# A tuned transformer kernel on one core: placing the side engines by a simulated timeline instead of the scheduler's default clock

## The chip, the cores and the metric

The kernel runs on one core of one Trainium2 chip. The metric is the device time of one execution in microseconds (us). Before the change the median of three timed runs is 2640.34 us (2638.31 to 2640.6). The profiled execution, from which every row below comes, took 2637.59 us; its span from the first to the last instruction is 2635.8 us.

## The reference

The input is 512 tokens of width 1024. The computation, all in fp32:

```
first block, on 16 meta tokens + 512 tokens:
  h = rmsnorm(x); split h @ w_in into the parts of
    FoX : 8 heads of 64, causal, softmax(q k^T * scale + cum[q] - cum[k]), times silu(gate)
    MLA : low-rank q (256) and kv (128), 8 heads, rope, chunk mask, softmax, times silu(gate)
  x = x + rmsnorm(concat(FoX, MLA) @ w_out)
two hybrid layers:
  h = rmsnorm(x); proj = h @ w_in
  A: mLSTM, 4 heads of 128, both directions, with a gate and a norm
  B: grouped-query attention, 8 query and 2 key heads of 64, rms norm of q and k, axial rope
  C: neighbourhood attention, 8 heads of 64, with a bias table
  D: differential attention, 4 heads, value width 128
  merged = sum over A..D of sigmoid(h @ w_gl) * (y @ w_up);   x = x + merged @ w_out
  x = x + (silu(h2 @ w_gate) * (h2 @ w_up)) @ w_down     with inner width 2816
final rms norm
```

## The kernel before

**Numbers.** Every operand of a large product is split into a high and a low half (`hi`, `lo`; `whi`, `wlo` for weights; `pth`, `ptl` for transposed attention maps), and a product is three TensorE passes: hi x whi, hi x wlo, lo x whi (`mm3` and its kin, L248 to L250, L296 to L298). So each weight tile of 128x512 that arrives by DMA (`raw`) passes two side engines before TensorE can use it, in `split_w`:

```
A_.copy(hi, src)                                                              # L220, ScalarE
k.turn += 1
(V if k.lo and k.turn % k.lo == 0 else G).tensor_tensor(lo, src, f(hi), ALU.subtract)   # L222
```

The subtraction is on GpSimd, except while branch B's queries are projected (`k.lo = 2`), where VectorE has every second one. `evict_split` does the same for results in PSUM: the cast on ScalarE (L210, L213), the subtraction on VectorE (L211, L214).

**Stages, in order of time (us of the span).** 0 to 34: loads, first norm (`norm_tile`, L503, L309, L310, L527) and its transposes. 34 to 200: projections and FoX. 200 to 308: MLA. 308 to 372: w_out of the first block with its two norms. 372 to 1470: layer 1 (A to about 540, B to 700, C to 870, D and merging to 1188, FFN after that). 1470 to 2636: layer 2, the same.

**The order of TensorE is written out by hand.** The whole body runs under `with tc.manual_schedule(engines={mybir.EngineType.PE})`: TensorE's instructions stand in the order in which the Python code issues them. `overlap` interleaves the stages of an attention map (scores, softmax, transposes, product with the values) with projection work from a `Stream` queue, by lags and credits (`LAG_F`, `LAG_M`, `TAIL`, `BETWEEN`, L32 to L40, L128). So the projection work is the filler under which a map's softmax runs on the side engines.

**The order of the other engines is not written out.** The tile framework's scheduler takes the instructions of VectorE (DVE), ScalarE (ACT), GpSimd (POOL) and SyncE (SP, which issues all large DMAs) and decides which comes next on each engine; an engine then runs its own list strictly in that order, and waits at the first instruction whose input is missing, with all that stand behind it. The scheduler's idea of when things are ready decides who stands ahead of whom.

**What the prediction's steps touch.** FoX: `p = A + cb` (L922, two pieces when the map is wider than 512), softmax (L331 max, L332 exp on ACT, L333 reciprocal), scale (L923), then transposes (L314), `pth`/`ptl` (L210, L211), product with the values (L443); after every second head `pair_out` (copy L446, two DMAs L452/L453, adds L454/L455), the gate (L931) and `split_y` (L459 ACT, L460 POOL). The score matmul (L721) of a later map takes over the PSUM bank that an earlier L922 has read. MLA: scale on ACT (L963) or DVE (L965), gate L977. First block's output: L1006, L1010, then `norm_tile`. Branch A: mask add L1336 and a power L1383 on POOL, normalisation L1378 to L1384. Branch B: norm and rope of the queries, `norm_rope` L1459 to L1468 with L309/L310, combination L1513/L1514; the merging `x = (g+1) * A` (L1148) of branch A's output runs beside it. Branch C: bias DMA L1630, bias add on POOL L1631, map L1636 to L1638, output split L1644/L1645, key stacks by DMA L390/L391.

The function that the change touches, and what calls it:

Of the kernel before, what the change touches and what calls it, by code (L numbers as in the profile page):

```python
# [1838 lines left out]
def build(nc, arrays):  # L1839
    aps = {}  # L1840
    for name, a in arrays.items():
        aps[name] = nc.dram_tensor(f"in_{name}_dram", a.shape, mybir.dt.from_np(a.dtype), kind="ExternalInput").ap()
    out = nc.dram_tensor("out_0_dram", (S, D), F32, kind="ExternalOutput").ap()
    with tile.TileContext(nc) as tc:
        hybrid_kernel(tc, aps, out)


# [9 lines left out]
```

## Time and profile before

| | before |
|---|---|
| median of three runs | 2640.34 us (2638.31 to 2640.6) |
| profiled execution, own time | 2637.59 us |
| its span | 2635.8 us |
| outside the span | 1.79 us |
| mean granted TensorE clock | 0.989 |
| TensorE busy | 2554.8 us, 97% |
| VectorE, ScalarE, GpSimd busy | 51%, 44%, 49% |
| DMA, mean over the span | 105 GB/s |

TensorE is busy for 97% of the span, so the time can change in two ways only: TensorE's waits (81 us in all, the span less its busy time) become shorter or longer, or the stretches in which its clock is granted at half change in number. The side engines are half idle on average, so their busy time says little; what counts is when single instructions of theirs end.

### The profile page before, as it was taken

Reading aid. Unit: us, or ns where it says so; the run is one execution under the profiler, and the core shown is the slowest. Engines: PE = TensorE matmul, PEld = TensorE weight load, DVE = VectorE, ACT = ScalarE, POOL = GpSimd, SP = SyncE. Lnnn points to the kernel's source line nnn. Section 1 sums busy time; section 2 is a strip of 40 time slices with the busy share of each in tenths; the row PEclk is TensorE's granted clock in tenths of the full one; section 3 lists DMA queues with packets and bytes.
Section 4 is the critical chain, followed back from the end, with each engine's and each line's share of the span. In section 5 each row is a group of like instructions: output and inputs, shape, how many; then the busy total and the mean of one; then the engine's idle time right before and its main releaser. Section 6 shows DMA issues by size and latency. Waiting matters only on the chain.

```text
span 2635.8 us, 36300 instructions
## 1 busy us (share of the span) xinstructions
PE 2554.8 (97%) x12918; PEld 2127.0 (81%) x12918; DVE 1334.6 (51%) x2895; ACT 1162.8 (44%) x2533; POOL 1291.5 (49%) x1112
## 2 busy tenths in 40 slices
PE   7999989999999999999999999999999999999998
PEld 7878778778887887788888887888888877888887
DVE  3677547858536466432222368685364573322223
ACT  4567645436534445332222454365454453322223
POOL 3443345442465543545555555524655535455554
PEclk9999999999999999999999999999999999999999
DMA  4542232222436332422222332223364233222222
GB/s 144 143 130 69 82 125 97 70 77 72 135 112 180 114 104 81 144 81 96 96 96 96 109 110 69 83 73 103 122 182 127 94 91 139 85 96 96 96 96 88
DMA packets 117732, 276.96 MB, mean 105 GB/s; under 512 B 15824, under 2 KB 37584, under 8 KB 117552
## 3 DMA queue, kind: packets, MB, share of 16 engines
q1 hardware_dynamic: 117552, 274.65, 33.2%
q8 instruction: 102, 1.67, 0.3%
q14 instruction: 78, 0.64, 0.1%
HBM read 230.26 MB, written 6.46 MB: 90 GB/s over the span
## 4 chain that ended last, share of the span: by engine, by line
PE 75%; DVE 10%; POOL 4%; issue 4%; DMA 3%; ACT 2%; SPq 0%; POOLq 0%; DVEq 0%; ACTq 0%
PE A L248 17%; PE A L249 16%; PE A L250 16%; PE A L296 5%; PE A L297 5%; PE A L298 5%; PE A L314 4%; PE A L443 3%; POOL wlo L222 2%; DMA raw<-in_w_out_dram 1%; DVE ptl L211 1%; DMA cb<-in_c_rpb_z_dram 1%; PE A L488 1%; DVE sm L331 1%; PE A L278 1%
## 5 line engine op out<-in xcount | busy, mean ns | idle before, releaser
L222 POOL TENSOR_TENSOR wlo<-raw,whi 128x512 fp32r<-128x512 f32 (+2 forms) x721 | 926.7, 1288 | 903.1 <-ACT whi L220 894.8
L220 ACT CAST whi<-raw 128x512 fp32r<-128x512 f32 (+2 forms) x733 | 443.9, 608 | 777.6 <-PE A L249 447.4
L248 PE MATMUL A<-hi,whi 128*128 128x512 f32 (+1 forms) x1848 | 744.3, 403 | 0.4 <-ACT hi L210 0.4
L250 PE MATMUL A<-hi,wlo 128*128 128x512 f32 (+1 forms) x1848 | 725.7, 393 | 10.3 <-DVE wlo L222 5.8
L249 PE MATMUL A<-lo,whi 128*128 128x512 f32 (+1 forms) x1848 | 727.0, 393 | 0.4 <-DVE lo L211 0.4
L250 PEld LDWEIGHTS A<-hi,wlo 128*128 128x128 f32 x1848 | 349.7, 189 | 91.0 <-DVE wlo L222 7.5
L248 PEld LDWEIGHTS A<-hi,whi 128*128 128x128 f32 x1848 | 350.4, 190 | 66.2 <-ACT whi L220 0.9
L249 PEld LDWEIGHTS A<-lo,whi 128*128 128x128 f32 x1848 | 350.3, 190 | 64.2 <-DVE lo L211 0.6
L314 PE MATMUL A<-ident,p 128*128 128x128 f32 (+3 forms) x1125 | 175.5, 278 | 28.1 <-DVE p L527 19.9
L497 DVE TENSOR_TENSOR x<-x,A 128x512 f32<-128x512 f32 x176 | 120.0, 688 | 154.0 <-PE A L298 96.8
L314 PEld LDWEIGHTS A<-ident,p 128*128 128x128 f32 (+3 forms) x1125 | 135.7, 139 | 67.2 <-DVE p L527 19.1
L211 DVE TENSOR_TENSOR ptl<-A,pth 128x512 fp32r<-128x512 f32 (+3 forms) x256 | 148.9, 583 | 80.0 <-ACT pth L210 78.9
L332 ACT ACTIVATE p<-p,sm 128x512 f32<-128x512 f32 (+6 forms) x160 | 100.7, 629 | 155.2 <-DVE sm L331 154.0
L354 DVE SCALAR_TENSOR_TENSOR t<-t,A 128x512 f32<-128x512 f32 x44 | 30.3, 688 | 252.7 <-ACT t L353 252.7
L210 ACT CAST pth<-A 128x512 fp32r<-128x512 f32 (+3 forms) x256 | 127.5, 502 | 54.6 <-PE A L314 54.2
L310 POOL TENSOR_TENSOR rstd<-rstd,mhalf 128x1 f32<-128x1 f32 (+2 forms) x80 | 56.0, 701 | 194.4 <-DVE rstd L309 187.8
L296 PE MATMUL A<-whi,hi 128*128 128x256 f32 (+7 forms) x440 | 145.9, 332 | 0.0
L297 PE MATMUL A<-wlo,hi 128*128 128x256 f32 (+7 forms) x440 | 143.1, 325 | 1.1 <-POOL wlo L222 1.1
L298 PE MATMUL A<-whi,lo 128*128 128x256 f32 (+7 forms) x440 | 142.9, 325 | 0.0
L1067 DVE SCALAR_TENSOR_TENSOR t<-A,t 128x512 f32<-128x512 f32 x44 | 30.4, 692 | 171.2 <-PE A L250 171.2
L296 PE MATMUL A<-whi,yh 128*128 128x512 f32 x288 | 112.1, 389 | 0.0
L297 PE MATMUL A<-wlo,yh 128*128 128x512 f32 x288 | 112.1, 389 | 0.0
(365 smaller groups left out, 4563.3 us busy)
## 6 DMA issues: line engine op xcount, KB each, us to landing
raw<-in_t_gl_dram SPq DMA_DIRECT2D x64, 512.0 KB, 3.5
raw<-in_t_gate_dram SPq DMA_DIRECT2D x44, 512.0 KB, 3.4
raw<-in_t_up_dram SPq DMA_DIRECT2D x44, 512.0 KB, 3.4
raw<-in_w_ffn_down_dram SPq DMA_DIRECT2D x44, 512.0 KB, 3.7
raw<-in_w_in_dram SPq DMA_DIRECT2D x26, 512.0 KB, 3.5
raw<-in_w_out_dram SPq DMA_DIRECT2D x24, 512.0 KB, 3.5
ks<-sth SPq DMA_DIRECT2D x64, 128.0 KB, 2.4
ks<-stl SPq DMA_DIRECT2D x64, 128.0 KB, 2.4
```

The source lines that it names most:

```text
L210: A_.copy(hi, ps)
L211: V.tensor_tensor(lo, ps, f(hi), ALU.subtract)
L220: A_.copy(hi, src)
L222: (V if k.lo and k.turn % k.lo == 0 else G).tensor_tensor(lo, src, f(hi), ALU.subtract)
L248: T_.matmul(ps, sh, mh, start=first, stop=False)
L249: T_.matmul(ps, sh, ml, start=False, stop=False)
L250: T_.matmul(ps, sl, mh, start=False, stop=last)
L296: T_.matmul(ps, sh, wh[:, j], start=(b + j == 0), stop=False)
L297: T_.matmul(ps, sh, wl[:, j], start=False, stop=False)
L298: T_.matmul(ps, sl, wh[:, j], start=False, stop=(b + j == nk - 1))
L314: T_.transpose(dst, src, ident[0:k, 0:k])
L497: V.tensor_tensor(xx, xx, ps, ALU.add)
```

## The change

One argument of the tile framework's context. With it the scheduler orders the instructions of the engines other than TensorE by a simulated timeline of engines and queues, where it went by its default clock before.

```
@@ -1841,7 +1841,7 @@
     out = nc.dram_tensor("out_0_dram", (S, D), F32, kind="ExternalOutput").ap()
-    with tile.TileContext(nc) as tc:
+    with tile.TileContext(nc, schedule_with_timeline_sim=True) as tc:
         hybrid_kernel(tc, aps, out)
```

No arithmetic changes. TensorE's list is the same, instruction for instruction. On the other engines the same operations stand in another order, over the whole program; on SP the order of some DMA issues changes too.

First place, VectorE in branch B of layer 1 (about 572 to 581 us of the trace). `wlo_6700` is the low half of a weight tile that TensorE's L250 waits for; `cb_6543` are queries in `norm_rope`; `x_4403` is the merged output; a row with + is new at this place, one with - has left it.

```order
 L1461 TENSOR_REDUCE bss_6649<-t_1402_6647 128x8
+L222 TENSOR_TENSOR wlo_6700<-raw_6697,whi_6699 128x512
 L309 TENSOR_SCALAR rstd_6651<-bss_6649 128x8
+L1148 SCALAR_TENSOR_TENSOR x_4403<-sth_4920,A_6636 128x512
 L1463 TENSOR_TENSOR cb_6543<-cb_6543,rstd_6651 128x512
-L1148 SCALAR_TENSOR_TENSOR x_4403<-t_1036_4919,A_6618 128x512
 L1464 TENSOR_TENSOR t_1401_6646<-cb_6543,cst_6067 128x512
 L1467 TENSOR_TENSOR t_1402_6647<-cb_6543,cst_6067 128x8x16 x4
-L222 TENSOR_TENSOR wlo_6700<-raw_6697,whi_6699 128x512
```

The subtraction L222 moves from behind L1463 to L1467 to a place ahead of L309. Layer 2 has the same piece with other numbers.

Second place, VectorE in FoX (about 148 to 155 us). `p_1835` is the map whose L922 frees a PSUM bank; the rows of `t_353` and `t_358` (L810 to L815) are the low-rank projections of MLA. Before:

```order
L309 TENSOR_SCALAR rstd_1768<-lss_1762 128x1
L815 TENSOR_SCALAR t_353_1759<-t_353_1759,rstd_1768 128x256
L211 TENSOR_TENSOR ptl_1687<-A_1749,pth_1686 128x4x128
L810 TENSOR_TENSOR t_359_1781<-t_358_1780,rope_774 128x16
L309 TENSOR_SCALAR rstd_1785<-lss_1783 128x1
L810 TENSOR_TENSOR t_359_1781<-t_358_1780,rope_774 128x16 x3
L815 TENSOR_SCALAR t_358_1780<-t_358_1780,rstd_1785 128x128
L309 TENSOR_SCALAR rstd_1789<-lss_1783 128x1
```

These eight rows stood one behind the other ahead of L922 of `p_1835`, with six more between the last of them and it. Now, at the same place:

```order
L309 TENSOR_SCALAR rstd_1764<-lss_1762 128x1
L211 TENSOR_TENSOR yl_171<-A_1689,yh_170 16x256
L309 TENSOR_SCALAR rstd_1768<-lss_1762 128x1
L922 TENSOR_TENSOR p_1835<-A_1831,cb_1661 128x400
L810 TENSOR_TENSOR t_359_1781<-t_358_1780,rope_774 128x16 x4
L815 TENSOR_SCALAR t_353_1759<-t_353_1759,rstd_1764 128x128
```

L922 of `p_1835` now stands directly behind the first of the eight; the low-rank work follows it.

Third place, ScalarE at the end of MLA (about 297 to 305 us). `p_3863` is the last map but one that L963 scales; `qs_3879` is the split of a gated head pair, whose input comes from L455 and L977 on VectorE.

```order
-L210 CAST yh_170<-A_3826 16x256
+L459 CAST qs_3879<-t_837_3873 128x512
 L210 CAST pth_3889<-A_3891 128x128
 L210 CAST yh_170<-A_3892 16x256
@@ -408,9 +410,8 @@
 L345 ACTIVATE p_3863,smb_3864<-A_3858,smb_3864 128x264
 L446 COPY t_845_3915<-A_3882 128x512
+L210 CAST pth_3917<-A_3919 128x3x128
 L963 ACTIVATE p_3863<-p_3863,smb_3864 128x528
-L459 CAST qs_3879<-t_837_3873 128x512
```

Here the cast L459, which has to wait for the gated pair, moves from behind L963 of `p_3863` to a place ahead of that map's casts and exponentials, and a cast of another map (`pth_3917`) moves ahead of L963.

## Rows read from the trace of the kernel before

**Rows 1.** Busy time of the engines on the page: us, share, instructions.

```profile
PE 2554.8 (97%) x12918; PEld 2127.0 (81%) x12918; DVE 1334.6 (51%) x2895; ACT 1162.8 (44%) x2533; POOL 1291.5 (49%) x1112
```

**Rows 2.** TensorE's waits: instruction <- releaser: us in total, times, longest us.

```profile
PE A L314 <- DVE p L527: 19.9, 9, 7.7
...
PE A L250 <- DVE wlo L222: 5.8, 2, 2.9
...
PE A L250 <- POOL wlo L222: 4.5, 2, 2.3
PE A L721 <- DVE p L922: 3.4, 2, 2.0
...
PE A L278 <- ACT whi L220: 1.2, 1, 1.2
...
PE A L278 <- POOL wlo L222: 0.9, 1, 0.9
```

**Rows 3.** TensorE's timeline, branch B, layer 1: start, duration, [idle before <- releaser].

```profile
580.98 0.50 PE L250 MATMUL A<-hi,wlo 128*128 128x512 f32 x1 [2.90 <-DVE wlo L222]
```

**Rows 4.** Timeline of ScalarE, the same stretch.

```profile
572.07 1.12 ACT L220 CAST whi<-raw 128x512 fp32r<-128x512 f32 x2
```

**Rows 5.** Timeline of VectorE, the same stretch.

```profile
576.54 1.77 DVE L1463 TENSOR_TENSOR cb<-cb,rstd 128x512 f32<-128x512 f32 x1 [2.86 <-POOL rstd L310]
...
580.24 0.68 DVE L222 TENSOR_TENSOR wlo<-raw,whi 128x512 fp32r<-128x512 f32 x1
...
586.22 0.69 DVE L1463 TENSOR_TENSOR yn<-yn,rstd 128x512 f32<-128x512 f32 x1 [1.91 <-POOL rstd L310]
```

**Rows 6.** Timeline of GpSimd, the same stretch.

```profile
576.48 1.29 POOL L222 TENSOR_TENSOR wlo<-raw,whi 128x512 fp32r<-128x512 f32 x1
```

**Rows 7.** PE, PEld, DVE, ACT, POOL busy (x count) by stretch, clock, DMA.

```profile
582.00:585.40 3.40, 3.40 (x13) 3.03 (x12) 2.24 (x6) 2.38 (x5) 1.83 (x2) 0.50 0.56 205
155.30:162.10 6.80, 6.80 (x22) 5.14 (x21) 4.66 (x15) 3.52 (x10) 1.19 (x1) 0.50 0.40 108
...
224.00:231.00 7.00, 6.39 (x45) 6.31 (x45) 6.14 (x23) 4.76 (x16) 1.70 (x2) 1.00 0.18 61
1715.20:1718.60 3.40, 3.40 (x13) 2.92 (x14) 3.12 (x7) 2.34 (x5) 0.84 (x1) 0.50 0.62 212
```

**Rows 8.** Timeline of TensorE in FoX.

```profile
148.24 0.61 PE L721 MATMUL A<-ks,qs 128*128 128x400 f32 x2
...
154.87 0.51 PE L721 MATMUL A<-ks,qs 128*128 128x264 f32 x2 [1.96 <-DVE p L922]
```

**Rows 9.** Timeline of VectorE in FoX, the same place.

```profile
154.24 0.57 DVE L922 TENSOR_TENSOR p<-A,cb 128x400 f32<-128x400 f32 x1
```

**Rows 10.** Timeline of VectorE at the end of FoX.

```profile
189.92 0.49 DVE L923 TENSOR_SCALAR p<-p,sm 128x528 f32<-128x528 f32 x1
...
193.68 1.52 DVE L931 SCALAR_TENSOR_TENSOR t<-t,yn 128x512 f32<-128x512 f32 x1
195.13 0.43 DVE L922 TENSOR_TENSOR p<-A,cb 128x272 f32<-128x272 f32 x1
```

**Rows 11.** Timeline of TensorE at the end of FoX.

```profile
195.61 1.37 PE L721 MATMUL A<-ks,qs 128*128 128x264 f32 x4 [1.46 <-DVE p L922]
```

**Rows 12.** Timeline of VectorE at the end of MLA.

```profile
304.06 0.67 DVE L977 SCALAR_TENSOR_TENSOR t<-t,yn 128x512 f32<-128x512 f32 x1
```

**Rows 13.** Timeline of ScalarE at the end of MLA.

```profile
304.27 0.74 ACT L963 ACTIVATE p<-p,smb 128x528 f32<-128x528 f32 x1
```

**Rows 14.** Timeline of TensorE at the end of MLA.

```profile
305.06 0.71 PE L314 MATMUL A<-ident,p 128*16 128x128 f32 x5 [0.87 <-ACT p L963]
```

**Rows 15.** Timeline of GpSimd in branch A of layer 1.

```profile
487.66 1.27 POOL L460 TENSOR_TENSOR ks<-t,ks 128x512 fp32r<-128x512 f32 x1
```

**Rows 16.** Timeline of GpSimd in branch C of layer 1.

```profile
857.68 1.58 POOL L1645 TENSOR_TENSOR yl<-t,yh 128x512 fp32r<-128x512 f32 x1 [2.58 <-ACT yh L1644]
```

**Rows 17.** Timeline of TensorE in branch C of layer 1.

```profile
857.49 0.40 PE L250 MATMUL A<-hi,wlo 128*128 128x512 f32 x1
```

More of the change, by code (lines that the diff above doesn't have):

```diff
@@ L1843, in build @@
     out = nc.dram_tensor("out_0_dram", (S, D), F32, kind="ExternalOutput").ap()
-    with tile.TileContext(nc) as tc:
+    with tile.TileContext(nc, schedule_with_timeline_sim=True) as tc:
         hybrid_kernel(tc, aps, out)
```

## Prediction

> **What bounds the kernel now.** I read the page first. TensorE is busy for 2554.8 of 2635.8 us [rows 1]; no other engine is above half, so the only time that an order of the side engines can move is the 81 us in which TensorE stands, and what its clock loses beside them. Then the list of TensorE's waits [rows 2]: it says which instruction waits for which, and so which place of which engine's order matters. The largest sums are norm tiles (L527: 19.9 us in nine waits, one of them 7.7 us at the very start, where the input still arrives), the low halves of weights made by L222 on VectorE (5.8 us in two waits) and on GpSimd (4.5 in two), and FoX's L922 (3.4 in two). Two at the start, for the first weights, are 1.2 and 0.9 us. Last I read the timelines of the waiting engine and of its releaser side by side, to see whether the releaser was late because its input was late or because it stood behind other work. Only the second kind can be won.
>
> **The clearest term: branch B, both layers.** TensorE's L250 starts at 580.98 after an idle time of 2.90 us [rows 3]. The cast of that weight's high half was done at 573.2: 572.07 + 1.12 [rows 4]. But VectorE made the low half at 580.24 [rows 5], because L1463 (576.54, after waiting for GpSimd's power) and what follows it stood ahead. In the new order L222 stands ahead of L309, so it can run at about 573.3 and end at 574.0; even if it took as long as the slow L1463, 1.77 us, it would end at 575.1. TensorE wants it at 578.1 (580.98 - 2.90). The wait goes: -2.9 in each layer, as the wait list counts two of them, 2.9 the longest. What was hidden before and might come out: L222's old place is ahead of nothing urgent, and L1148, which also moves forward (0.68 us class, like L222), fills time in which L1463 waits 2.86 us for GpSimd anyway. Bounds for the pair: 0 to -5.8.
>
> From 582.00 to 585.40 and from 1715.20 to 1718.60 the granted clock is 0.50, that is 1.2 of 2.4 GHz, with TensorE busy all the time [rows 7]; it had stood for 2.9 us just before either. The same work at the upper level takes half as long, so each such stretch costs 1.7 us. Not every stretch with idle time has it: 224 to 231 shows 1.00 although TensorE stands for 0.61 us of it. Here I take both stretches as gone: 2 x -1.7 = -3.4, bounds 0 and -3.4. Branch B in all: -9.2, and +0.5 for its attention maps, where the maximum L331 of a later map now stands ahead of a scale.
>
> At this place the Trainium skill speaks against the move. The trace first: L1463 takes 1.77 us when it starts 0.06 us behind GpSimd's L222 (576.48, 1.29 us), and 0.69 alone [rows 5, 6]; it ends 0.5 us after GpSimd's does. The page "SBUF — State Buffer" (section "SBUF: two separate sides") says that VectorE operations with two SBUF inputs and GpSimd share one port pair as an exclusive lock, where the loser waits for the whole instruction. The trace agrees with it here. By that rule a subtraction that VectorE takes earlier can also hold up GpSimd's, and I make a rival of it below; for this place the 3 us to spare cover one such wait of 1.08 us (1.77 - 0.69).
>
> **FoX at 155 us.** L721 starts at 154.87 after 1.96 us idle [rows 8], released by L922, which ran at 154.24 [rows 9]. Its input, the score matmul L721 at 148.24 with a mask behind it [rows 8], was there some 5 us earlier; thirteen rows of low-rank work, output splits and the like stood ahead of it, and in the new order they stand behind it. -2.0. From 155.30 to 162.10 the clock is 0.50 [rows 7]: another -3.4 if it goes too. Bounds 0 to -5.4; I take -5.4.
>
> **End of FoX: a loss.** L922 of `p_2342` moves forward here as well, and the idle 1.46 us before L721 at 195.61 [rows 11] would go. But what L922 passes is the scale L923 of `p_2268` (0.49, at 189.92) and that of `p_2302`, and the latter comes to stand behind L931, which took 1.52 [rows 10]. L931 (193.68 before) would run at about 194.2 to 195.7, with one L923 and a maximum more ahead of it; the scale of `p_2302` (0.3) ends at 196.0, its transposes (0.7, as in rows 14) at 196.7, and only then comes L721: +1.1 against 195.61. An earlier map's scale moves behind an L922 (0.43) and a maximum: +0.6. Together +1.7, with -1.5 (only the wait goes) and +3.5 (all scales wait in a row) as bounds.
>
> **End of MLA: a loss.** ScalarE's L459 must wait for L977, which ended at 304.73 [rows 12], and now stands ahead of the last maps' casts and exponentials. L977 has itself moved forward on VectorE, to an end at about 303.2 by the operations that it passes. Behind it on ScalarE then come a cast of 0.6, and what ran from 301.30 to 304.27 before L963 [rows 13]: packed, about 2.5 us. L963 starts at about 306.4 in place of 304.27, and the transposes at 305.06 [rows 14] come 2.1 later. Bounds: 0 if L977 is done before 301, and +4.1 if it is not earlier than before (304.73 + 0.6 + 3.0 - 304.27). Smaller shifts of the same kind in MLA, four of half a microsecond against two waits of a quarter that go: +0.5. A wait of over 2 us on TensorE was followed by a half-clock stretch in branch B, so I add one: +1.7. MLA in all +4.3.
>
> **Branch A, both layers.** GpSimd's L222 for the L250 that waits (4.5 us, two times) now goes ahead of L460 (1.27 at 487.66) [rows 15]; its own cast and a power ahead of it keep some of that: -0.9 each, bounds 0 and -1.27. Against this, the normalisation L1378 to L1381 is now spread between the reciprocal and the scales of later maps: +0.5 in each layer. Sum -0.8.
>
> **Start.** The two first casts of weights and their low halves go ahead of three casts of activations; L278 waits 1.2 and 0.9 us for them [rows 2]. Two subtractions (0.68 class) slip ahead of the first norms, which I put at +0.5. -1.6, bounds 0 and -2.1.
>
> **First block's output norms.** Two subtractions and two products go ahead of one norm tile and behind the next. I take 0, bounds plus and minus 2.2, the mean of the nine waits (19.9 / 9).
>
> **Branch C.** The bias DMAs are issued ahead of eight key-stack DMAs, and the bias adds follow; but GpSimd's output split, L1645, now stands ahead of a weight's L222. L1645 ran from 857.68 to 859.26 [rows 16], and the L250 that needs that weight started at 857.49 [rows 17]. Unless L1645 itself comes earlier, the low half is ready at 859.26 + 1.29 = 860.55, 3.1 late. Its input hangs on a pair sum that the earlier bias lets come sooner, by about as much; I take +0.5 for each layer, bounds -0.5 and +3.1.
>
> **Sum.** -1.6 - 5.4 + 1.7 + 4.3 + 0 - 0.8 - 9.2 + 0.5 + 1.0 = -9.5. Against the profiled execution's own 2637.59 (span 2635.8 and 1.79 outside) that gives 2628.1. The median of the timed runs stands 2.75 above that execution, so 2630.8.
>
> **Rivals.** (a) The clock does not come back. A half-clock stretch is there after some waits and not after others; if the waits shorten and all the stretches stay, 3.4 in FoX and 3.4 in branch B are not won: -2.7, 2637.6. For it: FoX's stretch covers work behind a wait of only 2.0 us. Against: in branch B it follows the largest waits. (b) Slower: an operation that waits for a late input now stands ahead of ready ones, in the three places where a head pair's sum comes back by DMA. C costs 3.1 plus 1.7 of clock in each layer (9.6), FoX's end 3.5 plus 1.7 in place of 1.7 (+3.5), MLA 4.1 in place of 2.1 (+2.0); against the sum, which has 1.0 for C, that is +14.1; with the first block's +2.2 it is +16.3, 2647.1. It decides once these places cost 14.8 more than I give them. For it: L459, L1645 and L455 really move ahead of ready work. Against: the DMA's return is itself earlier where the copies move forward. (c) The losses do not come, because the inputs of the moved operations are earlier throughout: without FoX's end, MLA and C the sum is -16.5, 2623.8. (d) Port collisions move to places that end a wait: 1.08 each, five of them give +5.4, 2636.2. L931's 1.52 in a FoX that shows other lengths for like work speaks for it; in branch B there is room. (e) The order does not matter at all, because TensorE's own list fixes the pace: the wait of 2.90 us beside an input ready 7 us earlier speaks against it, and I give it nothing of its own.
>
> **How the numbers follow.** The forecast has 0.60, (a) 0.14, (b) 0.12, (c) 0.07, (d) 0.07. A measurement of this kernel can tell about 0.2% (5.3 us) from no change, so faster means below 2635.1 and slower above 2645.6. The forecast and (c) are faster, 0.67; (a) and (d) fall within 0.2%, 0.21; (b) with its own tail is slower, 0.12. The range reaches from below (c)'s 2623.8, with the half-clock stretch of MLA and one more left out (2 x 1.7), to 2643, where half of what (b) adds is in: 2620 to 2643.
>
> **What would show it.** In the new profile the wait of L250 for VectorE's L222 is gone from the list, and 575 to 586 shows clock 1.00. L721's wait for L922 falls from 3.4 to under 1.5 in all. New or longer waits stand at L314 behind L923 near 193 and behind L963 near 305, under 2.5 each. TensorE's busy time falls by the clock's share, some 5 us, and its idle time by about 5. Wrong would be: the L222 wait still there, a wait of over 3 us for wlo in branch C, or a busy time that does not fall.

## The result, and the profile after

The changed kernel takes 2605.53 us (median of 4 runs, 2603.77 to 2611.06), the kernel before 2639.32 beside it (4 runs, 2633.2 to 2640.6): a ratio of 0.9877 with a 95% interval of 0.9863 to 0.9891, about 32 us faster. Forecast were 2630.8 us, with 2620 to 2643 as the range. The side was right; the gain is over three times the forecast, and the result lies 14 us below the range.

The line of busy times on the page after (us, share, instructions; before: [rows 1]):

```profile
PE 2538.1 (97%) x12918; PEld 2117.7 (81%) x12918; DVE 1335.3 (51%) x2895; ACT 1163.9 (45%) x2533; POOL 1291.9 (50%) x1112
```

The view of the cores after, span and mean granted clock of TensorE (before: 2635.8 us, 0.989):

```profile
core 0: 2608.8 us, clock 0.993
```

The side engines do the same work (within 1.1 us each). TensorE is busy for 16.7 us less and idle for 10.3 less (2608.8 - 2538.1 = 70.7, against 81.0). The busy time falls for the larger part because the clock is up for longer: time lost to the clock is the span times what is missing to 1.00, 29 us before (0.011 x 2635.8) and 18 after (0.007 x 2608.8).

TensorE's waits after (columns as in [rows 2]):

```profile
PE A L314 <- DVE p L527: 16.3, 5, 7.3
PE A L250 <- POOL wlo L222: 6.0, 5, 2.2
PE A L314 <- DVE p L923: 5.0, 2, 3.6
...
PE A L314 <- DVE t L1514: 4.4, 2, 2.3
...
PE A L1635 <- DMA ks<-stl: 1.0, 2, 0.6
```

The wait of L250 for VectorE's L222 (5.8 in [rows 2]) and that of L721 for L922 (3.4) are no longer in the list. Two lines are new: L314 waits for L1514 (branch B's rotated queries) and longer for L923 (FoX's scale). The wait of branch C for its key stacks (copies of the keys that DMAs put together) is short. The list of before has these two lines for it, a wait of which the prediction spoke nowhere:

```profile
PE A L1634 <- DMA ks<-sth: 3.3, 1, 3.3
PE A L1634 <- DMA ks<-stl: 2.2, 1, 2.2
```

TensorE has the same instructions in the same order in both kernels, so each place can be compared: from a matmul's start to a later one's, in the two profiled executions (own times 2637.59 and 2611.06). Worked out from the two timelines, us; the clock column is half of the change in time at clock 0.50:

| place (us before) | forecast | span | idle | clock |
|---|---|---|---|---|
| start, 0 to 34 | -1.6 | -3.3 | -1.5 | 0 |
| FoX, 120 to 170 | -5.4 | -5.2 | -2.0 | -3.4 |
| end of FoX, 170 to 205 | +1.7 | +1.1 | +2.0 | 0 |
| start of MLA, 205 to 230 | none | +4.6 | +1.6 | +3.4 |
| rest of MLA, 230 to 312 | +4.3 | +3.3 | +0.9 | +3.4 |
| first block's norms, 312 to 372 | 0 | -3.3 | -2.5 | 0 |
| A, both layers | -0.8 | -11.5 | -2.2 | -10.2 |
| B, both layers | -8.7 | -3.2 | -1.0 | -1.7 |
| C, both layers | +1.0 | -7.7 | -4.4 | -3.4 |
| all | -9.5 | -26.5 | -9.8 | -12.0 |

The medians lie farther apart than this pair (33.8 against 26.5), since the profiled execution of the changed kernel is the slowest of its four. The feed-forward parts are unchanged; the places that the table leaves out give about -1.3 together. The two columns do not make up the whole span: almost 5 us of the gain are busy time at clock 1.00, 1.8 of them at the start; what they come from stays open.

### The profile page after: what moved, and what is told of

Its sections match the earlier page's. It is cut to its first block, busy times and chain, and to the rows that moved or that the text cites. A ratio compares the mean times of both kernels' runs of the same rounds, so it can differ in the third digit from the quotient of the medians.

```text
span 2608.8 us, 36327 instructions
## 1 busy us (share of the span) xinstructions
PE 2538.1 (97%) x12918; PEld 2117.7 (81%) x12918; DVE 1335.3 (51%) x2895; ACT 1163.9 (45%) x2533; POOL 1291.9 (50%) x1112
## 3 DMA queue, kind: packets, MB, share of 16 engines
q8 instruction: 103, 1.69, 0.3%
## 5 line engine op out<-in xcount | busy, mean ns | idle before, releaser
L222 POOL TENSOR_TENSOR wlo<-raw,whi 128x512 fp32r<-128x512 f32 (+2 forms) x721 | 925.2, 1285 | 886.1 <-ACT whi L220 870.0
L220 ACT CAST whi<-raw 128x512 fp32r<-128x512 f32 (+2 forms) x733 | 445.0, 609 | 815.6 <-PE A L249 475.3
L248 PE MATMUL A<-hi,whi 128*128 128x512 f32 (+1 forms) x1848 | 741.0, 401 | 0.7 <-ACT hi L210 0.7
L250 PE MATMUL A<-hi,wlo 128*128 128x512 f32 (+1 forms) x1848 | 722.5, 391 | 6.0 <-POOL wlo L222 6.0
L250 PEld LDWEIGHTS A<-hi,wlo 128*128 128x128 f32 x1848 | 348.2, 188 | 85.6 <-POOL wlo L222 8.6
L248 PEld LDWEIGHTS A<-hi,whi 128*128 128x128 f32 x1848 | 348.5, 189 | 64.9 <-ACT hi L210 0.8
L314 PE MATMUL A<-ident,p 128*128 128x128 f32 (+3 forms) x1125 | 176.2, 279 | 31.3 <-DVE p L527 16.3
L211 DVE TENSOR_TENSOR ptl<-A,pth 128x512 fp32r<-128x512 f32 (+3 forms) x256 | 149.1, 583 | 89.9 <-ACT pth L210 88.7
L314 PEld LDWEIGHTS A<-ident,p 128*128 128x128 f32 (+3 forms) x1125 | 135.2, 139 | 71.5 <-DVE p L527 17.7
L310 POOL TENSOR_TENSOR rstd<-rstd,mhalf 128x1 f32<-128x1 f32 (+2 forms) x80 | 56.7, 710 | 175.5 <-DVE rstd L309 168.3
```

The source lines that it names most:

```text
L211: V.tensor_tensor(lo, ps, f(hi), ALU.subtract)
L248: T_.matmul(ps, sh, mh, start=first, stop=False)
L250: T_.matmul(ps, sl, mh, start=False, stop=last)
L314: T_.transpose(dst, src, ident[0:k, 0:k])
```

## The experiments

Nearly all have one mechanism. Edges without a semaphore are added after the kernel is built, so that one engine's instructions stand in the order of a list; nothing is computed otherwise. To the kernel that a run is made of:

```diff
+ORDER = [
...
+]
+def issue_order(tc, nc):
+    by = {i.name: i for i in nc.all_instructions()}
+    edge = mybir.DependencyInfo(mybir.DependencyClass.NoSync, mybir.DependencyReason.DATA)
+    for names in ORDER:
+        for first, then in zip(names, names[1:]):
+            tc.add_manual_dep(by[f"I-{then}"], f"I-{first}", edge, reason="order")
         hybrid_kernel(tc, aps, out)
+        issue_order(tc, nc)
```

Below only the lists are shown; a comment names what a number is. A ratio is always that to the kernel before, in runs on the same chip.

**One stage at a time.** Four kernels made of the kernel before: first the exchange on which the forecast rested most (branch B's L222), then the whole new order of one stage. The traces of the three stage kernels show another order of instructions in the named stretches alone.

```diff
+    [6702, 6652],    # DVE: L222 (wlo), L309; layer 1, and the same in layer 2
+    [17245, 17195],
```

> The kernel before, with one order edge in each layer: VectorE's subtraction L222 (the low half that L250 waited 2.9 us for) ahead of the L309 of the same place in branch B. Theory 1 (the prediction's): both waits of 2.9 us go and with them both half-clock stretches of 3.4 us, 2 x (2.9 + 1.7) = -9.2 us; GpSimd keeps its old order, so the new wait of L314 for L1514 (2.3 us in each layer of the changed kernel) should be smaller or absent: -9.2 to -6. Rival (the clock does not come back): -5.8 at most, with the half-clock stretches still there.

Measured: 2638.58 us, ratio 0.9997 (0.9986 to 1.0008). Theory 1 is out; the rival's bound holds, though its reason is not the one that the trace shows. The exchange is worth nothing. It did not stay quite alone, since the scheduler moved the next round's L222 and three products L1148 on VectorE, and one weight load on SyncE, along with it in each layer. The wait of 2.9 is gone, and TensorE stands later in the same stage; its idle time there is 4.71 and 5.07 us in the two layers, against 3.79 and 3.88 before (its timeline):

```profile
584.73 0.50 PE L250 MATMUL A<-yh,wlo 128*128 128x512 f32 x1 [0.67 <-DVE wlo L222]
591.84 0.51 PE L248 MATMUL A<-hi,whi 128*128 128x512 f32 x1 [0.85 <-ACT whi L220]
...
601.35 0.79 PE L248 MATMUL A<-hi,whi 128*128 128x512 f32 x1 [2.06 <-ACT whi L220]
```

The casts L220 stand behind L1513 on ScalarE, which belongs to the same rotary norms as before (ScalarE's timeline of this run):

```profile
600.07 0.71 ACT L1513 CAST t<-t 128x256 fp32r<-128x256 f32 x2 [5.79 <-DVE t L1468]
600.69 1.13 ACT L220 CAST whi<-raw 128x512 fp32r<-128x512 f32 x2
```

```diff
+    # DVE, ACT, POOL, SP: the changed kernel's order of what ran from 400 to 545 and 1534 to 1680 us
...
```

> The kernel before, with the changed order on VectorE, ScalarE, GpSimd and SyncE in branch A alone (400 to 545 and 1534 to 1680 us), by order edges. Theory 1 (every stage's change is made by the order in that stage): -11.5 us, the sum of the two stretches in the two traces, of which about 9 to 10 us are half-clock stretches that go. Rival (the branch got faster because it was entered with another state of buffers, queues and clock): near 0. The prediction's own figure for the order of this branch was -0.8.

Measured: 2622.72 us, ratio 0.9938 (0.9918 to 0.9957), so about -16 us; in its profile stage A is 14.6 shorter, 5.6 of it idle time and 10.2 clock.

```diff
+    # the same for 700 to 870 and 1834 to 2004 us
...
```

> The kernel before, with the changed order on the four side engines in branch C alone (700 to 870 and 1834 to 2004 us). Theory 1: VectorE's pair sum L455 goes ahead of maps, so the output split, the casts of weights and the release of the next weight load all come some 2 us earlier; the key-stack DMAs then no longer run beside a 512 KB load, and the waits of L1634 (3.3 and 2.2 us) go with their half-clock stretches: -7.7 us. Rival (the DMAs are earlier only because branch B ended earlier, and SyncE's own order hardly changes): the waits stay, 0 to -2 us.

Measured: 2626.42 us, ratio 0.9955 (0.9938 to 0.9972), about -12 us; stage C is 8.7 shorter in the profile. Another half-clock stretch that is missing there lies in FoX, which this kernel does not touch (last section).

```diff
+    # the same for 3 to 400 us
...
```

> The kernel before, with the changed order on the four side engines in the first block alone (3 to 400 us). Theory 1 (sum of this stretch in the two traces): start -3.3, FoX at 155 us -5.2, end of FoX +1.1, start of MLA +4.6, end of MLA +3.5, output norms -3.3, in all -2.9 us. Rival (single stretches depend on the execution: the half-clock stretches come and go by chance): any sum between -10 and +5, with other half-clock stretches than in the changed kernel.

Measured: 2632.77 us, ratio 0.9975 (0.9961 to 0.9989), about -6.6 us, with -2.9 to -10.3 as the interval; theory 1's -2.9 lies at its edge.

**Do they add, and what is B worth?** All stages but B, and B alone.

```diff
+    # the lists of the three stage kernels together: 3 to 545, 700 to 870, 1534 to 1680, 1834 to 2004 us
...
```

> Made of the kernel before: the changed kernel's order on all engines in the first block and MLA, in stage A of both layers and in stage C of both layers, and the order before everywhere else, branch B (545 to 700 and 1680 to 1834 us) among it. Theory 1 (the losses of the stages are separate, and branch B is worth nothing, since its chain of rotary norms sets its end in either order): the three stages alone gave -16.4, -11.9 and -6.6 us, in sum -35, so about 2604 us, as fast as the changed kernel or up to 3 us faster. Rival (the gains hang on each other, since what one stage leaves open on the other engines the next one pays, or the gains of the three were in part one and the same half-clock stretch): clearly less, 2612 to 2620 us.

Measured: 2610.38 us, ratio 0.9884 (0.9864 to 0.9904), about -31 us, of 35 when the three are added. That lies between the two theories, 6 us above the 2604 of the first and 2 below the 2612 of the rival: the three stages add within what the intervals can tell, and the difference from the changed kernel's 0.9877 is inside them too.

```diff
+    # 545 to 700 and 1680 to 1834 us
...
```

> Made of the kernel before: the changed kernel's order on all engines in branch B of both layers alone. Theory 1 (the chain of rotary norms sets the end of this stage, so only its collisions and the clock change): by the stage tables of before and after -2.5 us in the first layer and -0.9 in the second, about -3 in all, 2635 to 2637 us; the wait of L250 for L222 near 580 us gone, and TensorE waiting at L314 for the product L1514 instead, about 2 us in each layer. Theory of the prediction (the wait of 2.9 us and the half-clock stretch behind it are gained whole): -9.2 us, about 2630 us. Rival (the chain is lengthened by the collisions of GpSimd's L222 and L1631 with VectorE more than the wait was worth): slower than before by 1 to 4 us.

Measured: 2635.80 us, ratio 0.9984 (0.9973 to 0.9995), about -4 us, as theory 1 said; the interval ends at -7.1, short of the prediction's -8.7 (-9.2 and +0.5). The new wait is there:

```profile
604.64 1.06 PE L314 MATMUL A<-ident,t 128*128 128x128 f32 x8 [2.38 <-DVE t L1514]
```

**Not one execution's luck.** The clock comes and goes between executions (last section), so one pair of profiles can mislead. But the kernels of this document run most stages in either order, each with a profile of its own. Length of a stage in those profiles, and TensorE's idle time in it (both layers together for A to C), us:

| stage | order before: kernels, length, idle | changed order: kernels, length, idle |
|---|---|---|
| FoX, 120 to 170 | 7, 47.2 to 50.4, 2.0 | 8, 45.0, 0 |
| start of MLA | 7, 24.9 to 27.9, 2.2 to 2.3 | 5, 27.3 to 29.5, 2.9 to 3.9 |
| A | 6, 289.2 to 291.3, 15.1 to 18.5 | 7, 276.6 to 279.8, 9.5 to 13.4 |
| B | 7, 308.6 to 309.3, 7.5 to 9.2 | 4, 303.9 to 305.9, 6.5 to 7.0 |
| C | 6, 339.3 to 342.6, 6.9 to 9.2 | 7, 331.4 to 333.9, 1.2 to 3.1 |

The two groups are apart everywhere but at the start of MLA, where the 4.6 of the table of places is twice the distance of the middles (25.0 and 27.3). In stage A the idle time falls by about 5 us, not by the 2.2 of that table: in the six kernels with A's order before, the idle time is the longer the less the clock costs (15.1 us beside 11.9 of clock, 18.5 beside 5.1). So the two columns of that table are no independent terms: what one execution loses to its clock, another stands and waits for in part.

**What bounds B.** In the kernel before TensorE, held up by L222, comes to the transposes of L1514's product without a wait, at 605.46; the first wait had hidden a second one. Before, and after, on VectorE (last of four rounds of the queries' rotary norm; columns as in [rows 3]):

```profile
600.75 0.76 DVE L1514 TENSOR_TENSOR t<-t,t 128x256 f32<-128x256 f32 x2 [0.47 <-ACT t L1513]
```

```profile
587.98 1.77 DVE L1463 TENSOR_TENSOR yn<-yn,rstd 128x512 f32<-128x512 f32 x1 [1.75 <-POOL rstd L310]
589.78 1.67 DVE L1464 TENSOR_TENSOR t<-yn,cst 128x512 f32<-128x512 f32 x1
592.29 0.69 DVE L1468 TENSOR_TENSOR t<-t,t 128x512 f32<-128x512 f32 x1
593.51 0.76 DVE L1514 TENSOR_TENSOR t<-t,t 128x256 f32<-128x256 f32 x2 [0.53 <-ACT t L1513]
```

Each round is L1461, L309, GpSimd's L310 (1.64 us), L1463 to L1468, ScalarE's L1513, and the next round's square L1459 stands behind L1513. Counted from the stage's start, TensorE comes to these transposes 5.0 us sooner than before (55.2 in place of 60.2), and the product starts 1.2 us later, as the four rounds take 37.7 us in place of 36.5. Two kernels made of the changed one, one with a shorter way to the third round's L310 (the expectation calls it the second) and one with shorter rounds:

```diff
+    [6728, 8058, 6825],     # POOL: L310 (rstd), L1631 (cb), L222 (wlo); and the same in layer 2
+    [17271, 18601, 17368],
```

> Made of the changed kernel: on GpSimd in branch B of both layers the second round's L310 (the root of the norms, part of the chain) stands ahead of L631's neighbour L1631 and of an L222, behind which it stood. Theory 1 (the chain of rotary norms sets the end of branch B): L310 and what follows it start 1.5 to 2 us sooner, the wait of L314 for L1514 falls by 1 to 2 us in each layer, in all -2 to -4 us, 2601 to 2603 us. Rival (the late low halves then hold TensorE's L250 or L314 as long): within 1 us of the changed kernel.

Measured: 2607.36 us, ratio 0.9868 (0.9847 to 0.989): no difference from the changed kernel that can be told. The waits for L1514 fall only from 2.10 and 2.31 to 1.74 and 1.69, and new waits of L250 for L222, 0.36 and 0.38, take that back for the larger part, as the rival said.

```diff
-        V.tensor_tensor(dst, dst, tmp, ALU.add)
+        V.tensor_tensor(dst[:, :, 0:1], dst[:, :, 0:1], tmp[:, :, 0:1], ALU.add)
```

> Made of the changed kernel, with a part of the work left out: in branch B's rotary norm the last sum L1468 is taken over one head's 64 columns in place of 512 (0.69 us each), so that each of the three rounds of the queries is about 0.5 us shorter; the instructions and their order stay. Theory 1 (the chain of three rounds sets when L1514 is ready, and L314 waits for it 2.1 and 2.3 us): the wait falls by 1.0 to 2.1 us in each layer, -2 to -4 us in all, 2601 to 2604 us. Rival (the weights' copies and low halves, L220 and L222, hold TensorE as long as the chain does): the wait for L1514 falls but waits of L248 or L250 take its place, within 1 us of the changed kernel.

Measured: 2601.85 us, ratio 0.9868 (0.9852 to 0.9883), 0.0009 below the changed kernel's, which is inside the intervals. The trace decides here. The last round on VectorE:

```profile
588.48 0.69 DVE L1464 TENSOR_TENSOR t<-yn,cst 128x512 f32<-128x512 f32 x1
590.01 0.22 DVE L1468 TENSOR_TENSOR t<-t,t 128x64 f32<-128x64 f32 x1
590.76 0.76 DVE L1514 TENSOR_TENSOR t<-t,t 128x256 f32<-128x256 f32 x2 [0.53 <-ACT t L1513]
```

L1514 comes 2.75 us sooner against the changed kernel: 0.5 lies ahead of this stage, 1.3 are the shorter sums of the four rounds, and 1.0 is L1464, which takes 0.69 in place of 1.67. The order did not stay as the expectation has it: a cast L220 came to stand behind the last L1513 on ScalarE, and so GpSimd has no second L222 beside L1464. The chain is shorter in two ways, then; but no wait of TensorE for L1514 is left in either layer, and none of L248 or L250 takes its place. TensorE's idle time in stage B is shorter by 2.1 and 2.2 us. So the chain of four rounds is what bounds B once L222 is out of the way: the traces show it, the medians cannot tell so little.

**Stage A: one exchange or the whole order?** Made of the kernel before, the exchange that the forecast priced at 0.9 a layer:

```diff
+    [5822, 5660],      # POOL: L222 (wlo), L460 (ks); and the same in layer 2
+    [16365, 16203],
```

> Made of the kernel before by one exchange of two neighbours on GpSimd in stage A of each layer: L222 (low half of the weights that TensorE's L250 waits for near 490 us) ahead of L460 (low half of a key stack). Nothing else moves. Prediction's term: 0.9 us a layer, 1.8 us in all, 2637 us. Theory 1 (in stage A the wait is one of several, and the half-clock stretch of 3.4 us that stands behind it at 489.8 goes with it when the wait falls below what the chip answers with a lower clock): -1 to -5 us, 2634 to 2638 us, with L250's gap near 490 down from 2.25 to about 1 us. Rival (the exchange alone carries most of the 16 us that the whole order of stage A gave): 2622 to 2628 us.

Measured: 2638.68 us, ratio 0.9995 (0.9982 to 1.0009): nothing. TensorE's timeline, before and with the exchange:

```profile
490.21 0.80 PE L250 MATMUL A<-hi,wlo 128*128 128x512 f32 x1 [2.25 <-POOL wlo L222]
491.17 1.09 PE L314 MATMUL A<-ident,p 128*128 128x128 f32 x4 [0.16 <-DVE p L1366]
```

```profile
489.39 0.50 PE L250 MATMUL A<-hi,wlo 128*128 128x512 f32 x1 [1.01 <-POOL wlo L222]
491.59 0.98 PE L314 MATMUL A<-ident,p 128*128 128x128 f32 x4 [1.70 <-DVE p L1366]
```

The wait that shrinks by 1.24 is paid two matmul groups on, where the map's scale L1366 is now the late one (+1.54); layer 2 shows the same (2.24 to 1.01, and 0.47 to 1.69). In the whole new order both are smaller: L314 starts 1.54 us behind L250, not 2.20, because L1366 is sooner against L250. After:

```profile
486.71 0.50 PE L250 MATMUL A<-hi,wlo 128*128 128x512 f32 x1 [0.48 <-POOL wlo L222]
...
488.25 0.87 PE L314 MATMUL A<-ident,p 128*128 128x128 f32 x4 [1.03 <-DVE p L1366]
```

**Stage C: one instruction.** Made of the kernel before; on VectorE only L455 moves, by two places.

```diff
+    [8937, 8843, 8844, 8876],        # DVE: L455 (pair sum), L333, L1638, L211; and the same in layer 2
+    [19480, 19386, 19387, 19419],
```

> Made of the kernel before by moving one instruction of VectorE in stage C of each layer: L455 (the second half of the pair sum of t2_1926) ahead of L333 and L1638, right behind L454, as the changed kernel has it. Nothing else moves. Theory 1 (the wait of 3.2 and 3.1 us for the key stack's DMA at 807 and 1940 us comes from a chain L455, L1644, the weight casts, L222, the release of a weight slot, so that the 512 KB weight load is issued beside the key-stack DMAs instead of ahead of them): the weight load is issued 1 to 2 us sooner against TensorE's work, the wait falls by 1 to 3 us in each layer, and with it the half-clock stretch behind it in some executions; -3 to -9 us, 2630 to 2636 us. Rival (the rest of the stage's new order is needed, such as L1631 placed ahead of L222 on GpSimd): both waits stay, within 1.5 us of before.

Measured: 2635.05 us, ratio 0.9974 (0.9961 to 0.9987), about -7 us. VectorE and then SyncE's queue, before:

```profile
791.54 1.26 DVE L1638 TENSOR_SCALAR p<-p,sm 128x384 f32<-128x384 f32 x1
792.83 1.11 DVE L455 TENSOR_TENSOR t<-t,t 64x512 f32<-64x512 f32 x1
```

```profile
799.87 0.33 SPq L240 DMA_DIRECT2D raw<-in_t_dk_dram  x1
800.32 0.46 SPq L390 DMA_DIRECT2D ks<-sth  x1
...
804.18 0.60 SPq L390 DMA_DIRECT2D ks<-sth  x1
805.88 0.46 SPq L391 DMA_DIRECT2D ks<-stl  x1
```

With L455 moved:

```profile
789.89 1.67 DVE L455 TENSOR_TENSOR t<-t,t 64x512 f32<-64x512 f32 x1
791.79 0.59 DVE L1638 TENSOR_SCALAR p<-p,sm 128x384 f32<-128x384 f32 x1
```

```profile
797.47 0.33 SPq L240 DMA_DIRECT2D raw<-in_t_dk_dram  x1
799.11 0.46 SPq L390 DMA_DIRECT2D ks<-sth  x1
...
803.55 0.60 SPq L391 DMA_DIRECT2D ks<-stl  x1
```

L455 releases L1644 and the casts behind it on ScalarE, they release GpSimd's L222, and that frees the slot for the 512 KB weight load L240. Before, this load is issued 0.45 us ahead of the first key-stack DMA and lands at 805.86, and the last key-stack DMA goes out only then. Now it goes 1.64 ahead and lands at 800.93, and TensorE's wait falls from 3.25 to 0.17 in layer 1, the stage by 3.8 us:

```profile
807.46 0.55 PE L1634 MATMUL A<-ks,qs 128*128 128x256 f32 x1 [3.25 <-DMA ks<-sth]
```

```profile
803.47 0.36 PE L1635 MATMUL A<-ks,qs 128*128 128x256 f32 x1 [0.17 <-DMA ks<-stl]
```

In layer 2 the move does not bring the load forward against the key-stack DMAs (0.53 us ahead, before 0.48): a wait of 1.7 stays of 2.2, and the stage is as long as before. The rest of the stage's order takes that. All 15 profiled kernels have this place twice. Where the load goes out 0.43 to 0.53 us ahead of the first key-stack DMA, 13 times, TensorE waits 1.7 to 3.8 us; where it goes 0.67 to 2.03 ahead, 17 times, at most 1.1. So the wait hangs on the distance between the two issues.

**The losses in FoX and MLA.** Made of the changed kernel: the order before where it loses, and then a single cause.

```diff
+    # DVE, ACT, POOL, SP: the order before of what ran from 172 to 228 and 285 to 312 us
...
```

> Made of the changed kernel: on the engines other than TensorE the order before from 172 to 228 us (end of FoX and start of MLA) and from 285 to 312 us (end of MLA). Theory 1 (the late-landing operand of L454, placed ahead of ready copies, and the norm rows ahead of L977 are what the changed order loses there): the stage table shows +1.1, +4.6 and +3.5 us for these places, of which 6.8 us are half-clock time that can come in one execution and not in another; so between -2.5 (the waits alone) and -9 us, about 2597 to 2603 us. Rival (what follows has then less ready, and the first block's second half gives it back at 360 us): within 1 us of the changed kernel.

Measured: 2599.39 us, ratio 0.9844 (0.9827 to 0.9861) against 0.9877, 6 to 9 us faster than the changed kernel.

```diff
+    # DVE, ACT, POOL: the changed kernel's order from 205 to 330 us, but on DVE L454, L455 (2660, 2661) behind L211 of vm (2708)
...
```

> Made of the changed kernel by moving two instructions of VectorE at the start of MLA: L454 and L455 (pair sum of t2_551, which wait for a DMA that lands at 213.13 us) go behind the ready copies L211 of v and vm; the rest keeps the changed kernel's order there. Theory 1 (L454, waiting in the line ahead of ready copies, is the cause of the four new gaps at 215 to 219 us, 3.9 us in all, and of the half-clock stretch behind them): gaps L314 at 215.39 (1.42) and L721 at 216.93 (0.89) go, those behind shrink to about 1 us in all; -2 to -5 us against the changed kernel, 2600 to 2604 us. Rival (the copies of x that follow are then as late behind the pair sums, so the gap only moves): within 1 us of the changed kernel.

Measured: 2605.90 us, ratio 0.9874 (0.9846 to 0.9901): no difference that an interval of 14 us can tell. The cause on VectorE in the changed kernel, and the four waits of TensorE that follow:

```profile
213.22 1.51 DVE L454 TENSOR_TENSOR t<-t,t 64x512 f32<-64x512 f32 x1 [1.87 <-DMA t<-t]
214.66 0.67 DVE L211 TENSOR_TENSOR v<-A,v 128x512 fp32r<-128x512 f32 x1
```

```profile
215.39 0.64 PE L314 MATMUL A<-ident,ks 128*96 128x128 f32 x4 [1.42 <-DVE v L211]
216.93 0.30 PE L721 MATMUL A<-x,sth 96*128 96x144 f32 x1 [0.89 <-DVE v L211]
218.36 0.49 PE L721 MATMUL A<-x,sth 96*128 96x144 f32 x1 [1.13 <-DVE x L211]
219.30 0.49 PE L721 MATMUL A<-x,stl 96*128 96x144 f32 x1 [0.45 <-DVE stl L214]
```

VectorE has ready copies (L211 of `v`) and waits 1.87 us for a DMA. With the sums moved behind the copies of v the first two waits go, as theory 1 said, but the copies of x are then behind the sums, as the rival said:

```profile
218.21 0.33 PE L721 MATMUL A<-x,sth 96*128 96x144 f32 x1 [2.01 <-DVE x L211]
```

In sum the four waits of 3.9 become two of 2.6; the kernel before has 2.3 here. So by the trace the place of the two sums makes most of the idle time that the start of MLA lost; that is 1.3 us.

**Best of both.** Made of the changed kernel, with the stretches of mla_order_back and, among others:

```diff
+    # DVE at the start of MLA: L454, L455, L931 (2660, 2661, 2662) behind all copies
+    [4973, 4926], [15516, 15469],      # POOL: L222 (wlo), L1336
+    [6259, 6225], [16802, 16768],      # POOL: L1383, L460
+    [20213, 20141],                    # POOL: L222 (wlo), L1645
...
```

> Made of the changed kernel, to beat both: the order before from 172 to 228 and 285 to 312 us (as in mla_order_back), with these moves besides. VectorE's L454, L455 and L931 at the start of MLA behind all ready copies there; on GpSimd the L222 that L250 waits for at 403 and 1523 us ahead of an L1336 that waits for its DMA, the L310 of branch B's second round ahead of L1631 and an L222, an L1383 ahead of an L460 near 516 us, and an L222 ahead of an L1645 near 1951 us; on VectorE near 451 us the softmax products in the order before. Against mla_order_back (2599.4 us) theory 1 expects the waits of 1.5 (214 us), 1.6 and 1.3 (403 and 1523), 1.0 (452), 0.8 of 1.7 (520 and 1640) and 1.0 (1954) to go, -7 us of idle time, some of which shows up at the next wait: 2592 to 2598 us. Rival (what comes next is late by the same amount in most of these places): 2598 to 2602 us.

Measured: 2595.38 us (4 runs, 2594.1 to 2596.93), ratio 0.9845 (0.9828 to 0.9862): faster than the kernel before and than the changed one. Its runs and those of mla_order_back are of two chips, so the ratios count, and they are equal: nothing is shown to come on top of the order put back, as the rival said. At the start of MLA one wait of 0.28 and one of 1.21 are left.

```profile
PE 2534.2 (98%) x12918; PEld 2113.3 (82%) x12918; DVE 1341.6 (52%) x2895; ACT 1164.6 (45%) x2533; POOL 1295.3 (50%) x1112
```

Its TensorE is idle for 58.0 us (span 2592.2), 12.7 less than in the changed kernel.

## Why the prediction was right or wrong

**Right: the side, in part by luck.** The places other than A and C give -6.0 of the -9.7 that the sum has for them; that the whole is clearly faster comes from A and C, which it put near nothing.

**Right: FoX at 155.** L922 came forward past the rows ahead of it, the wait of 1.96 and the half-clock stretch went: -5.2 of -5.4. **Nearly right: the two losses that were named.** At the end of FoX +1.1 of +1.7, though the single wait at L314 behind L923 is 3.64 where under 2.5 was said: L454 and L455, which wait 1.47 and 1.01 us for their DMA, stand ahead of it. In the rest of MLA +3.3 of +4.3, with less wait and one more half-clock stretch than forecast. The start gave -3.3 of -1.6, but in the kernels with the order before this place alone varies from 24.6 to 28.0 us.

**Wrong: stage A, the step "-0.9 each ... Sum -0.8".** It priced one exchange; alone that exchange is worth nothing (0.9995), and the whole order of the stage is worth 16 us by the medians and about 12 by the profiles (A in the table of either order). The term was read from the one wait that has the largest sum, and other moves in the stage were not followed: in layer 2, L314's waits for L1288 (1.03), for `yn` behind L211 (0.68) and for L1367 (0.47) go as well. It also had no clock term. Before, the stretches behind the waits of stage A ran at clock 0.50 (columns as in [rows 7]):

```profile
489.80:496.60 6.80, 6.23 (x18) 4.77 (x19) 5.75 (x22) 1.70 (x4) 2.15 (x3) 0.50 0.23 80
...
1626.50:1629.90 3.40, 3.40 (x10) 2.63 (x10) 2.70 (x5) 1.06 (x3) 1.81 (x2) 0.50 0.18 74
```

After, in the stretches of stage A that hold these matmuls, the clock stays up (one half-clock stretch is left in the stage, at 412.6):

```profile
480.00:545.00 65.00, 61.66 (x362) 52.88 (x362) 51.80 (x146) 28.42 (x63) 36.90 (x34) 1.00 0.26 79
1560.00:1660.00 100.00, 95.26 (x542) 80.45 (x541) 84.79 (x239) 47.84 (x104) 57.13 (x53) 1.00 0.24 72
```

Which of the other moves in stage A carries how much was not tried.

**Wrong: stage C, "+1.0".** The step asked what L1645 would do to one L222, which cost nothing in layer 1 (in layer 2 a wait of 1.5 for that L222 came). What decided was the wait for the key-stack DMAs, 3.3 and 2.2 us in the list, which no step took up. It hangs on VectorE's L455 by four engines and a load, and c_one_l455_alone shows that: one instruction moved by two places gave 7 of the 12 us by the medians (3 to 10 by the interval), 3.8 of the 8.7 by the profiles, all of it in layer 1.

**Wrong: branch B, "-2.9 in each layer", with 1.7 of clock.** The wait went and 575 to 586 ran at clock 1.00, as was said (in layer 2 a half-clock stretch came behind the new wait, at 1713):

```profile
575.00:586.00 11.00, 11.00 (x57) 9.18 (x56) 8.34 (x15) 5.40 (x12) 5.52 (x4) 1.00 0.29 97
```

But the sentence on what was hidden and might come out looked only at L222's old place, and not at the next thing that TensorE needs. The rotary norms bound the stage a matmul group later, and most of the gain came back as the wait for L1514. The Trainium skill's page "SBUF — State Buffer" (section "SBUF: two separate sides"), by which a VectorE operation with two SBUF inputs and one of GpSimd lock each other out, had been weighed for the place of the wait, with 3 us to spare; rival (d) said that in branch B there is room. By the trace it told in this chain instead: L1463 1.77 and L1464 1.67, against 0.69 each, beside two L222 on GpSimd; L1463 took 1.77 here before as well, so L1464 is the new loss.

```profile
587.90 2.98 POOL L222 TENSOR_TENSOR wlo<-raw,whi 128x512 fp32r<-128x512 f32 x2
```

**Wrong: the norms of the first block, 0, and the start of MLA, not named.** The second norm tile, 3.02 us late before, is not late after (-3.3 in all). The start of MLA lost 4.6, 1.6 of it waits by rival (b)'s mechanism, an operation with a late input ahead of ready ones, and 3.4 a clock that falls there in some executions with the order before too; the rival named the mechanism for C, FoX's end and MLA's end. So (b) was real at FoX's end and at the start of MLA, and only its sum was outweighed.

**Sums that do not come out as written.** MLA's "four of half a microsecond against two waits of a quarter" is +1.5, not +0.5. The lower bound of 2620 takes MLA's half-clock stretch out twice, as (c) has no MLA left. The upper, 2643, has three quarters of what (b) adds in it, not half. None of the three would have brought the result into the range.

In sum the mechanisms (a wait goes if its releaser stood behind other work; a loss comes where a late input stands ahead) held; the sizes failed because single pairs of a wait and its releaser were priced, with little for what the rest of a stage's order does and with clock terms in three places only.

## What to carry to other kernels

A wait that vanishes is worth the distance to the next late thing that the waiting engine needs, not its own length: follow that engine two or three groups on, and read when each operand will be ready. Go through the whole list of waits, DMA waits too, and ask for each from which instruction it hangs, over engines and queue slots. Where a scheduler moves whole stages, run the stages apart: the three without B added to within 5 us here, and putting back the old order where the new one lost beat both.

## What was not expected of the hardware

The half-clock stretch does not follow from the wait alone. FoX's wait at L721 is 1.96 us in the kernel before, in a_order_alone and in c_order_alone, and the stretch behind it runs at clock 0.50 in the first two ([rows 7, 8]) and at 1.00 in the third. The windows of the latter two, from the wait's end on:

```profile
156.70:163.50 6.80, 6.80 (x24) 5.17 (x23) 4.36 (x15) 3.75 (x10) 0.81 (x1) 0.50 0.47 129
```

```profile
153.80:160.60 6.80, 6.80 (x46) 5.92 (x47) 5.75 (x18) 5.29 (x15) 1.27 (x1) 1.00 0.50 134
```

The third does 46 matmuls in the time of 24. So a clock term read from one execution is a chance, not a price: over 19 runs the kernel before spread from 2629.84 to 2645.58 us, 16 us, with one order of instructions. Why the chip lowers its clock in one and not in the other stays open. It is not chance alone: in the rest of MLA the clock stays at 1.00 in all seven kernels with the order before and falls in five of the six with the changed one. And it costs more in sum where there is more idle time: the eight kernels with 73.4 to 86.8 us of idle time have a mean clock of 0.988 to 0.992, the seven with 58.0 to 70.7 one of 0.993 to 0.998, though within either group the one does not follow the other.
